# A planner's two cost constants: the price of an f32r product, and the rate of a load

## The chip, the cores and the metric

The kernel runs on one core of a Trainium2 chip. The core has five engines with queues of their own: PE multiplies matrices, DVE and ACT do vector work, POOL does a few small operations, and SP issues the transfers from memory. Each engine executes its queue strictly in the order in which it was written; semaphores hold an instruction back until its inputs are there and its output buffer is free. The metric is the device time of one execution in microseconds (us), the median of three.

## What is computed

Two layers of an encoder on 256 tokens of width 1024, all in float32. Layer 0 mixes with a Hyena convolution (long convolution by Fourier products) and cross attention, then a dense SwiGLU. Layer 1 mixes with dilated attention in three groups and cross attention, then a mixture of eight experts, of which each token takes two. That last part, in outline:

```
def moe_swiglu(h, router, wg, wu, wd):
    logits = jnp.dot(hf, router)
    top_v, top_i = lax.top_k(logits, TOP_K)          # TOP_K = 2 of 8 experts
    gates = jax.nn.softmax(top_v, axis=-1)
    ...
    for each expert e, on the tokens that chose it:
        y = (jax.nn.silu(x @ wg[e]) * (x @ wu[e])) @ wd[e]
    out[token] += gate * y
```

The widths are D = 1024 and DFF = 2816, so that an expert has 3 x 1024 x 2816 weights, 34.6 MB. The eight experts are 277 MB of the 373 MB that the kernel reads and writes.

## The kernel before

**Precision by three products.** A float32 product is made of three products of the faster type f32r: each operand is split into a high part (ACT casts it) and a low part (DVE subtracts the high part from the whole), and `mm3` multiplies high by high, high by low and low by high. So each weight passes through three engines before PE can use its low part: SP loads a *unit* (128 x 2048 floats, 1 MiB), ACT casts it in two halves of 128x1024, DVE makes the low half of each, and PE multiplies.

**An expert.** Its 33 units are used in blocks of six: four units of gate and up columns (48 products of 512 columns), then two units of the down matrix (24 products) for the block before. Between them lie `act`: SiLU on ACT, a product on DVE, four transposes of 128 columns on PE, and the split of their result by ACT and DVE (the cast to 128x512, called `aT` below). There are 8 x 33 = 264 such units, and they fill the second half of the run.

**The plan.** The kernel is not issued as it is written down. `Plan.add` records every operation with its duration by `Plan.cost`; `Plan.order` then plays the whole program forward with these durations, a list scheduler for five engines, a transfer queue, eight PSUM banks and 24 slots of 1 MiB in SBUF, and writes down in which order each engine starts its operations and which slot each buffer takes. `Plan.flush` emits the operations in that order. All of them are issued from one line (L299 of the profile), so the profile's groups are told apart by their tiles: `s` is a buffer in a slot, `b` a PSUM bank, `kt` holds the identity matrix for transposes (`b<-kt,s` is a transpose).

**What the durations decide.** At each moment of the played time an engine takes, of the operations that are ready and whose buffers fit, the one that is due first. A load is issued as soon as a slot can be spared (`fits`, the branch for kind "stream") and the played transfer queue holds less than BACKLOG = 6 us. A slot that is set free goes to the end of a list, and the next buffer takes the slot at its front. On the chip nothing of the played time is left except the orders and the slots: a load waits until the last user of its slot, as the plan has dealt it, is done. At most N_SPLIT = 4 slots hold split weights at a time.

The two prices that the change touches stand in `cost`: the load's bytes by 360e3 (bytes per us), and the f32r product's columns by 2.4 per ns and a fixed 2.5 ns.

Of the kernel before, what the change touches and what calls it, by code (L numbers as in the profile page):

```python
# [119 lines left out]
class _Eng:  # L120
# [3 lines left out]
    def __getattr__(self, fn):  # L124
# [3 lines left out]
LAT = {("tensor", "tensor"): 0.0, ("vector", "vector"): 0.07, ("scalar", "scalar"): 0.1, ("gpsimd", "gpsimd"): 0.1,  # L128
       ("scalar", "vector"): 0.13, ("vector", "scalar"): 0.17, ("scalar", "tensor"): 0.27, ("vector", "tensor"): 0.25}
FREE = 0.2  # L130
TABLES = {AF.Exp, AF.Silu, AF.Sin}
LOAD = 1.3
ISSUE, LAND = 1.2, 14.0
# [2 lines left out]
class Plan:  # L136
# [182 lines left out]
    def cost(self, eng, fn, a, kw, aps):  # L319

        n = max((self.width(x) for x in aps), default=1)
        if fn == "add_rows":
            return ISSUE
        if fn == "dma_start":
            ap = aps[0]
            return self.width(ap) * ap.ap[0][1] * 4 / 360e3
        if eng == "tensor":
            if fn == "transpose":
                return 0.109
            r = kw["rhs"]  # L330
            n = self.width(r.on(r.t.ref))
            if kw["rhs_dt"] == F32R:
                return max(0.107, 0.0025 + n * 0.4167e-3)
            return 4 * max(0.054, 0.0025 + n * 0.4167e-3)
        if eng == "scalar":
            ptr = isinstance(kw.get("scale"), View) + isinstance(kw.get("bias"), View)
            return 0.05 + 0.834e-3 * n + 0.2 * ("accum_out" in kw) + 0.09 * ptr
        if eng == "vector":
            return 0.07 + (6.4e-3 if fn == "reciprocal" else 1.04e-3) * n + 0.06 * (fn == "scalar_tensor_tensor")
        if kw.get("op") == OP.pow:  # L340
            return 0.35 + 0.16 * n
        return 0.05 + 2.3e-3 * n if fn == "tensor_tensor" else 0.05 + 3.5e-3 * n if fn == "tensor_copy" else 0.05
# [52 lines left out]
    def order(self):  # L395
# [35 lines left out]
        while done < len(ops):  # L431
# [23 lines left out]
            for e in engines:  # L455
# [36 lines left out]
                else:  # L492
# [3 lines left out]
                    f = op.args[2] if op.fn == "activation" else None  # L496
                    if f in TABLES and f != table:
                        table, end = f, end + LOAD
                        busy[e] = end
                heapq.heappush(events, busy[e])  # L500
                for m in op.mems:
                    m.left -= 1
                    m.end = max(m.end, end)
                    if not m.left and m.kind != "at" and not m.pinned:
                        heapq.heappush(frees, (m.end + FREE, len(out), len(frees), m))
                        heapq.heappush(events, m.end + FREE)
                        self.n_split -= m.split
# [1126 lines left out]
```

## Time and profile before

| | us |
|---|---|
| median of 3 runs | 1332.57 |
| lowest and highest | 1332.44, 1333.93 |
| the profiled execution | 1331.97 |
| its span in the trace | 1330.1 |

The span is cut in the trace at the first and the last instruction; 1.9 us of the execution lie around it. The rows quoted below are of this execution. The profile has a page (busy time of each engine, and the same in 40 slices of the span), a chain of waits (what the end waited for, followed back), lists of instructions by shape, lists of waits, windows (busy time and count of instructions in a stretch), and a timeline. A matmul's record in them lasts longer than the distance to the next one, since matmuls are pipelined: the pace of PE is read from counts over a stretch, not from the mean duration.

### The profile page before, as it was taken

The page shows a single profiled execution, that of the slowest core. Times are in us where ns is not written, and L with a number is a line of the kernel's source. Part 1 is how long each engine was busy: PE and PEld are TensorE (multiplying, and loading weights), DVE is VectorE, ACT ScalarE, POOL GpSimd, SP SyncE. Part 2 cuts the span into 40 slices and gives each one's busy share as a digit, 9 for nine tenths or more (in the row PEclk, how much of TensorE's full clock was granted, in tenths as well). Part 3 has the DMA queues.
Part 4 walks back from the last instruction along what each step waited for, and adds up shares of the span by engine and source line. Part 5 has one row for each costly group of instructions (what it writes and reads, how often), then busy time and mean ns, then how long its engine had stood idle before and what let it go on. Part 6 is the DMA issues. An engine that isn't in the chain of part 4 may idle for free.

```text
span 1330.1 us, 16843 instructions
## 1 busy us (share of the span) xinstructions
PE 1307.0 (98%) x6256; PEld 1073.6 (81%) x6256; DVE 1077.9 (81%) x1429; ACT 895.7 (67%) x1190; POOL 41.3 (3%) x38
## 2 busy tenths in 40 slices
PE   6999999999999999999999999999999999999997
PEld 4798888888878888888888888888888778777775
DVE  7989775554578777898999989999988888988886
ACT  7455754444566566687877777876876777777774
POOL 0100000000001000000000000000000000000000
PEclk9999999999999999999999999999999999999999
DMA  9548533357435456299999999999999999999992
GB/s 370 222 146 293 212 138 129 134 187 271 173 127 207 126 172 248 97 371 354 341 375 348 342 367 356 356 375 360 336 365 368 364 351 345 376 360 351 368 354 77
DMA packets 57437, 372.84 MB, mean 280 GB/s; under 512 B 6415, under 2 KB 10595, under 8 KB 13700
## 3 DMA queue, kind: packets, MB, share of 16 engines
q1 hardware_dynamic: 56196, 367.49, 73.8%
q0 software_dynamic: 1152, 4.19, 1.7%
q8 instruction: 51, 0.84, 0.2%
q14 instruction: 38, 0.31, 0.1%
HBM read 365.88 MB, written 5.79 MB: 279 GB/s over the span
## 4 chain that ended last, share of the span: by engine, by line
PE 88%; issue 7%; ACT 2%; DMA 1%; DVE 1%; SPq 0%; POOL 0%; POOLq 0%; ACTq 0%; DVEq 0%
PE b L299 88%; ACT s L299 2%; DVE s L299 1%; DMA out<-s,tiny 1%; DMA sm<-sm 0%; SPq L299 0%; POOL out L296 0%; POOLq L1375 0%; DVE tiny L299 0%; ACTq L299 0%; DVE cg L299 0%; POOLq L296 0%; DVEq L299 0%
## 5 line engine op out<-in xcount | busy, mean ns | idle before, releaser
L299 PE MATMUL b<-s,s 128*128 128x512 f32 (+1 forms) x5674 | 1279.0, 383 | 2.9 <-DVE s L299 0.9
L299 PEld LDWEIGHTS b<-s,s 128*128 128x128 f32 x5674 | 1003.9, 188 | 215.3 <-DVE s L299 15.0
L299 DVE TENSOR_TENSOR s<-s,s 128x1024 fp32r<-128x1024 f32 (+3 forms) x729 | 832.7, 1187 | 124.5 <-ACT s L299 123.6
L299 ACT CAST s<-s 128x1024 fp32r<-128x1024 f32 (+1 forms) x705 | 689.8, 1039 | 128.6 <-PE b L299 96.6
L299 DVE TENSOR_TENSOR s<-b,s 128x512 f32<-128x512 f32 (+5 forms) x206 | 123.0, 609 | 63.4 <-ACT s L299 58.9
L299 ACT CAST s<-b 128x512 fp32r<-128x512 f32 (+3 forms) x118 | 58.3, 504 | 130.5 <-PE b L299 127.4
L299 ACT ACTIVATE s<-b 128x512 f32<-128x512 f32 (+3 forms) x81 | 42.9, 539 | 68.7 <-PE b L299 68.6
L299 PE MATMUL b<-kt,s 128*128 128x128 f32 (+1 forms) x480 | 88.1, 273 | 1.2 <-DVE s L299 1.0
L299 PEld LDWEIGHTS b<-kt,s 128*128 128x128 f32 x480 | 65.1, 146 | 18.6 <-ACT s L299 2.2
L299 ACT ACTIVATE s<-b,tiny 128x512 f32<-128x512 f32 (+2 forms) x58 | 34.0, 611 | 28.0 <-PE b L299 20.7
L299 DVE SCALAR_TENSOR_TENSOR s<-b,sm,s 128x256 fp32r<-128x256 f32 (+1 forms) x88 | 38.0, 478 | 8.2 <-ACT s L299 6.6
L299 ACT ACTIVATE s<-b,sm 128x256 fp32r<-128x256 f32 (+1 forms) x84 | 35.2, 487 | 11.9 <-PE b L299 11.4
L296 POOL DMA_INDIRECT out<-s,tiny x8 | 14.4, 1794 | 761.3 <-ACT s L299 569.5
L299 POOL TENSOR_TENSOR tiny<-tiny,mhalf 128x1 f32<-128x1 f32 (+4 forms) x23 | 26.5, 1152 | 341.5 <-DVE tiny L299 327.1
L299 ACT ACTIVATE s<-x 128x512 f32<-128x512 f32 x16 | 10.1, 631 | 17.7 <-DVE x L299 13.5
L299 PE MATMUL b<-s 128*128 128x512 f32 (+4 forms) x40 | 11.9, 389 | 10.0 <-DMA s<-fw 5.9
L299 DVE TENSOR_TENSOR tiny<-tiny 128x1 f32<-128x1 f32 (+4 forms) x81 | 12.2, 156 | 10.2 <-ACT s L299 8.3
L299 DVE TENSOR_REDUCE tiny<-b 128x2 f32<-128x512 f32 (+3 forms) x25 | 12.3, 495 | 9.5 <-PE b L299 9.4
L299 DVE TENSOR_REDUCE tiny<-s 128x4 f32<-128x512 f32 (+3 forms) x26 | 13.9, 558 | 5.3 <-ACT s L299 5.3
L299 PEld LDWEIGHTS b<-s 128*128 128x128 f32 (+2 forms) x40 | 6.7, 195 | 11.6 <-DMA s<-fw 5.9
L299 DVE TENSOR_TENSOR x<-b,x 128x512 f32<-128x512 f32 x12 | 8.3, 691 | 9.1 <-PE b L299 9.0
L299 ACT COPY s<-b 128x512 f32<-128x512 f32 x11 | 6.3, 584 | 13.6 <-PE b L299 13.4
(65 smaller groups left out, 157.4 us busy)
## 6 DMA issues: line engine op xcount, KB each, us to landing
s<-w_moe SPq DMA_DIRECT2D x264, 1024.0 KB, 7.1
s<-w_ffn SPq DMA_DIRECT2D x33, 1024.0 KB, 4.9
s<-w_at SPq DMA_DIRECT2D x20, 1024.0 KB, 5.1
s<-w_kv SPq DMA_DIRECT2D x8, 1024.0 KB, 7.9
s<-w_hy SPq DMA_DIRECT2D x8, 1024.0 KB, 16.3
s<-w_out SPq DMA_DIRECT2D x8, 1024.0 KB, 4.9
s<-mem SPq DMA_DIRECT2D x4, 512.0 KB
out<-x SPq DMA_DIRECT2D x3, 512.0 KB
```

What stands on the lines that cost most here:

```text
L296: self.nc.gpsimd.indirect_dma_start(out=out, out_offset=bass.IndirectOffsetOnAxis(ap=index, axis=0), in_=rows, in_offset=None, compute_op= ...
L299: getattr(getattr(self.nc, op.eng), op.fn)(*args, **kw)
```

## The change

Three lines. The fixed part of an f32r product goes from 2.5 to 13.7 ns, and its floor from 107 to 110 ns: 512 columns cost 227.05 ns in place of 215.85, 256 columns 120.4 in place of 109.2. A load costs its bytes by 390e3 in place of 360e3 per us: a unit of 1,048,576 bytes 2.689 us in place of 2.913. No operation is added, removed or changed; the orders and the slots are what the plan makes of these numbers.

```
+RATE = 390e3
...
         if fn == "dma_start":
             ap = aps[0]
-            return self.width(ap) * ap.ap[0][1] * 4 / 360e3
+            return self.width(ap) * ap.ap[0][1] * 4 / RATE
...
             if kw["rhs_dt"] == F32R:
-                return max(0.107, 0.0025 + n * 0.4167e-3)
+                return max(0.11, 0.0137 + n * 0.4167e-3)
             return 4 * max(0.054, 0.0025 + n * 0.4167e-3)
```

Every engine's order differs nearly everywhere. Two places of the last expert show it; the lines count from L299 before and L300 after, since one line was added. Behind a buffer's slot number stands a running number that is given out as the instructions are written.

The first place is ACT, around the cast of a block's transposes (128x512, from a bank). The casts to 128x1024 are of weights: on the right of the arrow stands the unit that was loaded. Before:

```order
L299 CAST s2_10348<-s20_10274 128x1024
L299 CAST s11_10354<-s20_10274 128x1024
L299 CAST s15_10365<-b7_74 128x512
L299 CAST s18_10370<-s6_10296 128x1024
L299 CAST s0_10377<-s6_10296 128x1024
L299 CAST s4_10389<-s8_10316 128x1024
```

After:

```order
L300 CAST s16_10375<-s2_10118 128x1024
L300 CAST s9_10385<-s2_10118 128x1024
L300 CAST s1_10393<-s14_10147 128x1024
L300 CAST s10_10402<-s14_10147 128x1024
L300 CAST s7_10414<-b1_68 128x512
L300 CAST s15_10418<-s21_10165 128x1024
L300 CAST s11_10426<-s21_10165 128x1024
```

Two things have moved. The unit behind the 128x512 cast was loaded 74 running numbers ahead of its cast before (10296 to 10370) and 253 ahead after (10165 to 10418); a unit takes some 20 of them, so that is 3 to 4 units ahead before and about 13 after. And the casts that stand in front of the 128x512 cast are further ahead of PE, which the second place shows.

The second place is PE, from the last transpose of the same block (`b<-kt`) to the first product with the weights that are cast next behind the 128x512 cast (s18_10370 before, s15_10418 after). Before:

```order
L299 MATMUL b7_74<-kt_77,s1_10277 128x128
L299 MATMUL b6_73<-s2_10348,s14_8883 128x512
L299 MATMUL b6_73<-s2_10348,s22_8916 128x512
L299 MATMUL b6_73<-s2_10348,s14_8883 128x512 x2
L299 MATMUL b6_73<-s2_10348,s22_8916 128x512
L299 MATMUL b6_73<-s11_10354,s14_8883 128x512 x2
L299 MATMUL b6_73<-s11_10354,s22_8916 128x512
L299 MATMUL b6_73<-s11_10354,s14_8883 128x512 x2
L299 MATMUL b6_73<-s11_10354,s22_8916 128x512
L299 MATMUL b6_73<-s18_10370,s14_8883 128x512 x2
```

After:

```order
L300 MATMUL b1_68<-kt_77,s13_10333 128x128
L300 MATMUL b3_70<-s16_10375,s4_9029 128x512
L300 MATMUL b3_70<-s16_10375,s20_9044 128x512
L300 MATMUL b3_70<-s9_10385,s4_9029 128x512 x2
L300 MATMUL b3_70<-s9_10385,s20_9044 128x512
L300 MATMUL b3_70<-s9_10385,s4_9029 128x512 x2
L300 MATMUL b3_70<-s9_10385,s20_9044 128x512
L300 MATMUL b0_67<-s1_10393,s7_10414 128x512 x3
L300 MATMUL b4_71<-s1_10393,s7_10414 128x512 x3
L300 MATMUL b0_67<-s10_10402,s7_10414 128x512 x3
L300 MATMUL b4_71<-s10_10402,s7_10414 128x512 x3
L300 MATMUL b0_67<-s15_10418,s7_10414 128x512 x3
```

Before, 11 products lie between the last transpose and the first product that needs weights cast behind it; after, 20.

## Rows read from the trace of the kernel before

**Rows 1.** The page: busy time, share and instructions of PE; its granted clock in slices.

```profile
PE 1307.0 (98%) x6256; PEld 1073.6 (81%) x6256; DVE 1077.9 (81%) x1429; ACT 895.7 (67%) x1190; POOL 41.3 (3%) x38
...
PEclk9999999999999999999999999999999999999999
```

**Rows 2.** The chain of waits in order of time: start us, us, what.

```profile
57.77 1.03 ACT s L299 x2
58.82 1.27 DVE s L299 x3
...
102.30 1.05 ACT s L299
...
103.40 928.16 PE b L299 x4457
...
1061.08 14.64 PE b L299 x64
...
1076.23 1.06 ACT s L299
1077.31 1.24 DVE s L299
1078.59 14.68 PE b L299 x64
```

**Rows 3.** Windows: length, busy us (count) by engine, PEclk, DMA share, GB/s.

```profile
575.00:1000.00 425.00, 425.00 (x1956) 352.48 (x1955) 386.05 (x394) 329.64 (x378) 8.18 (x4) 1.00 0.95 358
1000.00:1300.00 300.00, 298.05 (x1331) 237.79 (x1330) 259.79 (x264) 217.86 (x253) 4.63 (x3) 1.00 0.96 360
...
10.00:40.00 30.00, 28.70 (x112) 18.97 (x113) 28.60 (x71) 25.25 (x48) 2.27 (x4) 1.00 1.02 417
1040.00:1050.00 10.00, 9.73 (x45) 7.68 (x44) 8.50 (x9) 6.69 (x9) 0.00 (x0) 1.00 1.01 428
```

**Rows 4.** PE by shape, 318 to 358 us: xcount, busy us, mean ns, idle us.

```profile
L299 PE MATMUL b<-s,s 128*128 128x512 f32 x178 | 40.5, 389 | 0.0
```

**Rows 5.** The same, 575 to 1000 us.

```profile
L299 PE MATMUL b<-s,s 128*128 128x512 f32 x1784 | 417.1, 392 | 0.0
```

**Rows 6.** The same, 1000 to 1300 us.

```profile
L299 PE MATMUL b<-s,s 128*128 128x512 f32 x1223 | 294.7, 396 | 2.0 <-DVE s L299 0.7
```

**Rows 7.** Waits, 1000 to 1300 us: who <- whom, us, times, longest.

```profile
ACT s L299 <- PE b L299: 83.1, 37, 4.5
...
PEld b L299 <- DVE s L299: 12.4, 28, 0.7
```

**Rows 8.** Timeline of one block: start us, us, engine, operation, count, [idle before <-releaser].

```profile
1288.89 0.27 PE L299 MATMUL b<-kt,s 128*128 128x128 f32 x1
...
1289.20 0.59 ACT L299 CAST s<-b 128x512 fp32r<-128x512 f32 x1 [3.66 <-PE b L299]
1289.68 3.89 ACT L299 CAST s<-s 128x1024 fp32r<-128x1024 f32 x4
...
1292.04 5.31 PEld L299 LDWEIGHTS b<-s,s 128*128 128x128 f32 x24 [0.54 <-DVE s L299]
...
1297.72 0.30 PEld L299 LDWEIGHTS b<-s,s 128*128 128x128 f32 x2 [0.36 <-DVE s L299]
```

**Rows 9.** DMA issues, 575 to 1000 us: xcount, KB each, us to landing.

```profile
s<-w_moe SPq DMA_DIRECT2D x143, 1024.0 KB, 7.3
```

**Rows 10.** ACT by shape, 575 to 1000 us: the casts of weights.

```profile
L299 ACT CAST s<-s 128x1024 fp32r<-128x1024 f32 x300 | 295.1, 1050 | 23.9 <-PE b L299 17.7 <-DVE s L299 5.7
```

**Rows 11.** Waits of SP's queue, 575 to 1000 us.

```profile
SPq L299 <- PE b L299: 230.5, 96, 5.2
SPq L299 <- DVE s L299: 136.4, 75, 4.3
```

**Rows 12.** Waits of SP's queue, 1000 to 1300 us.

```profile
SPq L299 <- DVE s L299: 158.9, 74, 4.0
SPq L299 <- PE b L299: 97.0, 40, 5.2
```

More of the change, by code (lines that the diff above doesn't have):

```diff
@@ L130 @@
 FREE = 0.2
+RATE = 390e3
 TABLES = {AF.Exp, AF.Silu, AF.Sin}
@@ L325, in cost @@
             ap = aps[0]
-            return self.width(ap) * ap.ap[0][1] * 4 / 360e3
+            return self.width(ap) * ap.ap[0][1] * 4 / RATE
         if eng == "tensor":
@@ L332, in cost @@
             if kw["rhs_dt"] == F32R:
-                return max(0.107, 0.0025 + n * 0.4167e-3)
+                return max(0.11, 0.0137 + n * 0.4167e-3)
             return 4 * max(0.054, 0.0025 + n * 0.4167e-3)
```

## The prediction

> **What bounds the kernel now.** The page comes first: PE is busy for 98% of the span, at the higher of its two clocks, 2.4 GHz, in every slice [rows 1] (1.00 in the windows [rows 3]). So PE is the bound, and only its gaps and its pace can be won or lost. The chain of waits says where gaps are: after some waits in the first 103 us it is PE without a break from 103.40 to 1031.56 us (4457 products), and from there it breaks about once in 15 us, each time with an ACT and a DVE instruction of weight-split length in the break (1076.23, 1077.31), before PE goes on for 64 products [rows 2].
>
> Since a busy PE is not yet PE at its pace, I count products. The stretch from 318 to 358 us holds nothing but 512-column products: 178 in 40.5 us, 227.5 ns each [rows 4]. That is the new constant (227.05), not the old one (215.85). From 575 to 1000 us there are 1956 PE instructions in 425 us, 1784 of them of 512 columns [rows 3, 5]: 1784 x 227.5 ns = 405.9 us, which leaves 19.1 us for the 172 small ones, 111 ns each. From 1000 to 1300 us there are 1331 in 300 us, 1223 of 512 columns [rows 3, 6]: 278.3 us, and 108 small ones at 111 ns make 12.0, together 290.3. **9.7 us of these 300 are lost**, on the measure of the stretch before, and both stretches are the same work, experts.
>
> Why there? In the second stretch PE's weight loads wait 28 times for DVE, 12.4 us in all [rows 7], a wait that the first stretch doesn't list at all. One block shows the ring: the last transpose starts at 1288.89; ACT has idled 3.66 us for it and casts it at 1289.20, and only behind it, at 1289.68, come the casts of the next weights; PE gets the low half at 1292.04, after 0.54 us of waiting, and waits again for 0.36 at 1297.72 [rows 8]. From the transpose to 1292.04 are 3.15 us, and PE has 11 products to fill them, 2.5 us. ACT could have cast those weights earlier, had the order let it.
>
> **What the change does, part by part.** Nothing is computed otherwise; the plan's view of the experts turns over. A block of six units is 72 products and four transposes. By the old prices PE needs 72 x 0.2158 + 4 x 0.109 = 16.0 us for it, and the loads 6 x 2.913 = 17.5: the plan thinks that loads bound, runs its stock of loaded units down, and casts each just before its use. By the new prices PE needs 72 x 0.2271 + 4 x 0.11 = 16.8 us and the loads 6 x 2.689 = 16.1: PE bounds, the slots stay full, casts run ahead. The order bears this out at the end of the program: the unit behind the transposes' cast is loaded 3 to 4 units ahead before, about 13 ahead after, and PE has 20 products to cover that cast where it had 11.
>
> *The pace of loads.* The trace shows the old plan's draining on the chip: from 575 to 1000 us 143 units are loaded [rows 9] and 150 are cast (300 halves) [rows 10], so the stock falls by 7. It falls because of the slots that the plan has dealt, not because transfers are slow: SP's queue waits 230.5 + 136.4 of the 425 us for PE and DVE, that is for slots [rows 11], and 158.9 + 97.0 of 300 afterwards [rows 12]. To feed PE without a gap, 6 units in 16.8 us, takes 374 GB/s. The long stretches show 358 and 360, but the stretch from 10 to 40 us shows 417 and that from 1040 to 1050, in the midst of the experts, 428 [rows 3]. So 374 can be had when loads are issued earlier, and the 13 units of stock would cover a shortfall: at 360 GB/s a block's loads take 17.5 us, 0.7 more than PE, so that the stock loses a unit in four blocks and 13 units last 52 blocks, while all experts together have 264/6 = 44. Cost of the loads' part: nothing, hidden by that stock.
>
> The Trainium skill (DMA: Bandwidth & Descriptors, section Bandwidth, Where 436 GB/s comes from) says that for transfers from HBM the limit of some 358 GB/s per core binds. By that rule the two long stretches were at the limit and the change could not speed the experts up at all; this is the second rival below, which stands on rows 3 alone. The same skill (HBM Reference, Specifications (TRN2)) says that a core that streams alone reaches about 425, and this kernel runs alone; the 417 and 428 of the trace agree.
>
> *PE's and ACT's orders in the experts.* 20 products are 4.5 us against the 3.15 us of the ring, so the gap closes. What remains is what the first stretch shows, where the old plan still had its stock: the 111 ns for small instructions contain it. So the stretch from 1000 to 1300 us gets 9.7 us shorter. The bounds are +0 (the stalls stay) and about 12.4 (the whole wait for DVE [rows 7]); I take 9.7 because it is counted against the same work with a stock of loaded units. The rest of the experts after 1300 us goes on in the same way and I leave it out.
>
> *Everything before 575 us.* The price of PE moves every order there too. From 103 us on the chain is PE alone [rows 2], so there is next to nothing to win. In the first 103 us three breaks are in the chain, 1.03 + 1.27 and 1.05 us [rows 2], 3.3 in all: these can go, or as many of the same size can arise. I take 0, with 3 us to either side.
>
> *Pace.* The product's price in the plan doesn't change its time: 227.5 ns before and after. The skill (TensorE: Matmul & The Clock Gate, Back-to-back issue gap) gives N/2.4 + 2.5 ns for a warm, isolated product, 216 for 512 columns, the old constant. By that the new plan would be the one that misjudges PE; rows 4 decide for 227.5.
>
> **The sum.** The profiled execution took 1331.97 us; less 9.7 is 1322.3. The median of the runs lies 0.6 above the profiled one, so 1322.9, with 3 us either way: 1319.5 to 1326.
>
> **Rivals.**
>
> 1. *The stalls go only in part.* The ring from a transpose through ACT and DVE is in the new order too, and not every block has 20 products in it; where it has 11 to 14, PE can wait as it does now. For it: the orders are made by a scheduler that knows no fixed distance. Against: the old order has distances as short (9 products at the least) between 575 and 1000 us too, where the stock is larger, and the rows show no wait from them. If half of the 9.7 us stays: 1327.7.
>
> 2. *The transfers are the bound.* If 358 to 360 GB/s are all that a long stretch yields, the units come no sooner than now, the stock only shifts the gaps to the end, and PE waits for loads instead of DVE. For it: 358 and 360 over 425 and 300 us, at a DMA share of 0.95 and 0.96 [rows 3]. Against: the waits of SP's queue for slots [rows 11, 12], and 417 and 428 in the shorter stretches [rows 3]. It gives 1332, no change.
>
> 3. *The slots become the bound (slower).* With 13 to 14 loaded units in 24 slots, and 4 with split weights, few are left for an expert's activations. Then a cast or a SiLU on ACT waits for its slot, that is for a DVE or PE instruction that is late by plan, and all casts of weights queue behind it on ACT; PE waits in every block from the first expert on, not only from 1000 us. Price: the 9.7 us now lost are in 1223/72 = 17 blocks, 0.57 us each; if all 44 blocks lose that, 25.1 us take the place of 9.7, +15.4, 1348. It decides against the change from the point at which more than 17 of the 44 blocks wait as long as now. Against: in the old plan the stock is as large shortly after 575 us (it falls by 7 units until 1000 us [rows 9, 10], to 3 or 4), and PE has no break there [rows 2].
>
> That the change does nothing is ruled out by the orders.
>
> **How the numbers follow.** What a measurement of this kernel can tell from no change is 0.2%, 2.7 us: faster means under 1329.9. My forecast, 1319.5 to 1326: 0.71. Rival 1, 1326 to 1329.5: 0.13. Rival 2, 1330 to 1334: 0.09. Rival 3, above 1335: 0.07. Faster is the forecast and rival 1, 0.84; no change is rival 2, 0.09; slower is rival 3, 0.07. The range for 8 in 10 takes in the forecast and most of rival 1: 1318.5 to 1329.5.
>
> **What would show it.** Right: the chain is PE without a break from some 100 us to the end of the experts; from 1000 to 1300 us PE executes about 1375 instructions (1331 x 300/290.3) where it executed 1331; weight loads no longer wait for DVE there; the loads run at 370 to 375 GB/s in long stretches, and loaded units and cast units keep step. Rival 1: the wait for DVE is still listed, at some 6 us. Rival 2: the loads stay at 360 GB/s, and ACT or PE waits for transfers near the end. Rival 3: ACT waits for PE or DVE in every block from 575 us on. Wrong in a way that I have not priced: the breaks of the first 103 us grow by more than 3 us.

## The result, and the profile after

The changed kernel takes 1325.87 us (median of 4 runs, 1325.09 to 1326.87), beside 1333.05 us for the kernel before: a ratio of 0.9946, 95% interval 0.9929 to 0.9963. That is 7.2 us less; 9.7 were forecast. Run again later, it took 1325.09 beside 1333.24 (0.9941, 0.9928 to 0.9955). The profiled execution took 1326.87 us with a span of 1325.0, so the two profiles lie only 5.1 us apart.

The page after, PE's busy time and its granted clock in slices, beside [rows 1]:

```profile
PE 1304.2 (98%) x6256; PEld 1076.4 (81%) x6256; DVE 1083.5 (82%) x1429; ACT 907.6 (68%) x1190; POOL 43.1 (3%) x38
...
PEclk9999999999999999999999999999999999999999
```

The chain of waits after (start us, us, what), beside [rows 2]:

```profile
12.86 49.40 PE b L300 x252
62.34 292.57 PE b L300 x1473
...
357.66 1.47 POOL tiny L300
...
378.51 2.71 POOL tiny L300
...
383.95 190.56 PE b L300 x1009
574.51 613.43 PE b L300 x2812
```

Two things are to be seen. The breaks from 1031 us on are gone: PE runs from 574.51 to 1187.94 without one, and where the chain goes over to other engines behind that, PE stays busy all the same (300.00 of the 300 us up to 1300, below). The breaks of the first 103 us are gone too; the prediction counted three, but its rows are three instructions in two breaks. But there are two that the kernel before does not have, around 357 and 380 us, and in both a POOL instruction is the longest piece. PE itself idles for less than the chain is away from it: 0.39 us in the first, 0.88 and 0.19 us in the second.

The windows of the experts after (length, busy us and count of PE, PEld, DVE, ACT, POOL, then PEclk, DMA share, GB/s), beside [rows 3]:

```profile
575.00:1000.00 425.00, 425.00 (x1950) 350.41 (x1949) 387.15 (x396) 332.03 (x375) 6.48 (x4) 1.00 0.96 370
1000.00:1300.00 300.00, 300.00 (x1370) 246.64 (x1368) 271.43 (x273) 236.04 (x265) 4.76 (x3) 1.00 0.89 347
```

PE's 512-column products after, from 318 to 358, 575 to 1000 and 1000 to 1300 us (count, busy us, mean ns, idle us), beside [rows 4 to 6]:

```profile
L300 PE MATMUL b<-s,s 128*128 128x512 f32 x178 | 40.5, 389 | 0.0
...
L300 PE MATMUL b<-s,s 128*128 128x512 f32 x1775 | 416.9, 392 | 0.0
...
L300 PE MATMUL b<-s,s 128*128 128x512 f32 x1262 | 295.5, 392 | 0.0
```

The pace is what it was: 178 in 40.5 us. From 1000 to 1300 us PE now executes 1370 instructions where it executed 1331. By the prediction's measure (227.5 ns each for 1262, 111 ns for the other 108) that is 299.1 us of work in 300, so 0.9 are lost where 9.7 were.

The waits from 1000 to 1300 us after (who <- whom, us, times, longest), beside [rows 7]:

```profile
ACT s L300 <- PE b L300: 30.4, 45, 3.1
...
PEld b L300 <- DVE s L300: 0.8, 5, 0.2
```

The weight loads waited 12.4 us for DVE there before, and 0.8 now. A block late in the program (start us, us, engine, operation, count), beside [rows 8]:

```profile
1269.83 0.38 PE L300 MATMUL b<-kt,s 128*128 128x128 f32 x2
1270.08 11.93 PEld L300 LDWEIGHTS b<-s,s 128*128 128x128 f32 x53
1270.08 12.12 PE L300 MATMUL b<-s,s 128*128 128x512 f32 x52
1272.48 0.57 ACT L300 CAST s<-b 128x512 fp32r<-128x512 f32 x1
1272.95 1.05 ACT L300 CAST s<-s 128x1024 fp32r<-128x1024 f32 x1
```

The cast behind the transposes starts 2.7 us after they did and the weight cast behind that one at 1272.95; PE goes through 52 products without noticing either.

Loads and weight casts from 575 to 1000 us after, beside [rows 9, 10]:

```profile
s<-w_moe SPq DMA_DIRECT2D x148, 1024.0 KB, 7.6
...
L300 ACT CAST s<-s 128x1024 fp32r<-128x1024 f32 x296 | 297.8, 1051 | 78.6 <-DVE s L300 43.8 <-PE b L300 34.1
```

148 units are loaded and 296 halves, that is 148 units, are cast: the stock no longer falls. SP's queue still waits for slots (251.6 us for PE and 109.1 for DVE, beside [rows 11]), and the transfers give 370 GB/s where they gave 358.

To cut each trace in two I use one mark that all kernels have, four small products of the router (16x8 in the list), which stand close to the start of the experts. Before and after (start us, us, engine, operation, count):

```profile
548.69 0.61 PE L299 MATMUL b<-kt,s 16*128 16x8 f32 x4
```

```profile
551.16 0.61 PE L300 MATMUL b<-kt,s 16*128 16x8 f32 x4
```

Up to the mark the changed kernel is 2.5 us **later** (551.16 - 548.69). Behind it the span has 773.8 us left where it had 781.4 (1325.0 - 551.16 and 1330.1 - 548.69): 7.6 us shorter. The two make up the 5.1 us between the profiles.

### The profile page after: what moved, and what is told of

Its sections match the earlier page's. It is cut to its first block, busy times and chain, and to the rows that moved or that the text cites. A ratio compares the mean times of both kernels' runs of the same rounds, so it can differ in the third digit from the quotient of the medians.

```text
span 1325.0 us, 16885 instructions
## 1 busy us (share of the span) xinstructions
PE 1304.2 (98%) x6256; PEld 1076.4 (81%) x6256; DVE 1083.5 (82%) x1429; ACT 907.6 (68%) x1190; POOL 43.1 (3%) x38
## 4 chain that ended last, share of the span: by engine, by line
PE 88%; issue 7%; DVE 2%; DMA 2%; ACT 1%; POOL 0%; SPq 0%; POOLq 0%; DVEq 0%; ACTq 0%
PE b L300 88%; DVE s L300 2%; ACT s L300 1%; DMA out<-s,tiny 1%; DMA kt<-consts 1%; POOL tiny L300 0%; DVE tiny L300 0%; SPq L300 0%; POOL out L297 0%; DVE x L300 0%; POOLq L1376 0%; POOLq L297 0%; DVEq L300 0%; ACTq L300 0%
## 5 line engine op out<-in xcount | busy, mean ns | idle before, releaser
L300 PE MATMUL b<-s,s 128*128 128x512 f32 (+3 forms) x5676 | 1275.5, 382 | 5.1 <-ACT s L300 4.1
L300 PEld LDWEIGHTS b<-s,s 128*128 128x128 f32 (+1 forms) x5676 | 1007.0, 188 | 211.2 <-issue 6.7
L300 DVE TENSOR_TENSOR s<-s,s 128x1024 fp32r<-128x1024 f32 (+2 forms) x732 | 840.0, 1185 | 137.1 <-ACT s L300 133.7
L300 ACT CAST s<-s 128x1024 fp32r<-128x1024 f32 (+2 forms) x705 | 704.3, 1038 | 250.0 <-PE b L300 145.6
L300 DVE TENSOR_TENSOR s<-b,s 128x512 f32<-128x512 f32 (+5 forms) x206 | 123.1, 607 | 31.9 <-ACT s L300 27.7
L300 ACT CAST s<-b 128x512 fp32r<-128x512 f32 (+3 forms) x118 | 58.6, 504 | 55.1 <-PE b L300 53.1
L300 PE MATMUL b<-kt,s 128*128 128x128 f32 (+1 forms) x480 | 86.2, 277 | 1.2 <-DMA kt<-consts 0.6
L300 PEld LDWEIGHTS b<-kt,s 128*128 128x128 f32 x480 | 65.1, 148 | 19.9 <-issue 2.4
L300 ACT ACTIVATE s<-b 128x512 f32<-128x512 f32 (+3 forms) x81 | 43.3, 538 | 15.2 <-PE b L300 10.2
L300 ACT ACTIVATE s<-b,tiny 128x512 f32<-128x512 f32 (+2 forms) x58 | 33.7, 609 | 27.3 <-DVE tiny L300 16.3
L300 ACT ACTIVATE s<-b,sm 128x256 fp32r<-128x256 f32 (+1 forms) x84 | 34.6, 481 | 17.6 <-PE b L300 17.0
L300 DVE SCALAR_TENSOR_TENSOR s<-b,sm,s 128x256 fp32r<-128x256 f32 (+1 forms) x88 | 38.0, 477 | 10.6 <-ACT s L300 10.5
L300 POOL TENSOR_TENSOR tiny<-tiny,mhalf 128x1 f32<-128x1 f32 (+4 forms) x23 | 29.8, 1295 | 341.2 <-DVE tiny L300 341.2
L300 ACT ACTIVATE s<-x 128x512 f32<-128x512 f32 x16 | 10.1, 631 | 19.5 <-DVE x L300 13.7
L300 DVE TENSOR_REDUCE tiny<-b 128x2 f32<-128x512 f32 (+3 forms) x25 | 12.4, 495 | 11.8 <-PE b L300 11.7
L300 DVE TENSOR_TENSOR tiny<-tiny 128x1 f32<-128x1 f32 (+4 forms) x81 | 12.7, 158 | 9.6 <-POOL tiny L300 5.4
L300 DVE TENSOR_REDUCE tiny<-s 128x4 f32<-128x512 f32 (+3 forms) x26 | 14.2, 557 | 3.3 <-ACT s L300 3.3
L300 PE MATMUL b<-s 128*128 128x512 f32 (+3 forms) x38 | 11.0, 367 | 5.9 <-DMA s<-fw 5.9
L300 DVE TENSOR_TENSOR x<-b,x 128x512 f32<-128x512 f32 x12 | 8.2, 690 | 9.0 <-PE b L300 8.9
L300 DVE TENSOR_TENSOR s<-b,tiny 128x512 f32<-128x512 f32 (+3 forms) x26 | 13.9, 560 | 0.3
L300 ACT ACTIVATE s<-s,tiny 128x256 f32<-128x256 f32 (+1 forms) x24 | 13.0, 583 | 1.3 <-DVE tiny L300 1.3
```

The costliest lines, as they stand in the source:

```text
L300: getattr(getattr(self.nc, op.eng), op.fn)(*args, **kw)
```

## The experiments

The theory has two parts. (a) The late gain comes from the plan no longer letting the stock of loaded units run out; whichever price eases the balance of a block will do. (b) The front lost time by its new order, with POOL's powers in the two new breaks. All kernels at a glance; the ratio is to the kernel before, run in the same job (a job is a set of kernels run together), and the last two columns are the mark in the profiled execution and the rest of its span.

| kernel | median us | ratio | interval | to the mark | rest |
|---|---|---|---|---|---|
| before | 1333.05 | 1 | | 548.7 | 781.4 |
| after | 1325.87 | 0.9946 | 0.9929 to 0.9963 | 551.2 | 773.8 |
| new_late | 1323.92 | 0.9936 | 0.9920 to 0.9953 | 549.6 | 772.6 |
| new_early | 1334.91 | 1.0013 | 1.0004 to 1.0023 | 550.1 | 783.4 |
| rate_only | 1322.62 | 0.9928 | 0.9911 to 0.9944 | 549.5 | 771.5 |
| price_only | 1325.07 | 0.9952 | 0.9935 to 0.9968 | 549.4 | 773.2 |
| rate330 | 1343.99 | 1.0078 | 1.0061 to 1.0095 | 552.4 | 791.1 |
| after_gap | 1326.69 | 0.9944 | 0.9927 to 0.9960 | 552.0 | 773.8 |
| before_gap | 1334.17 | 1.0004 | 0.9994 to 1.0014 | 549.7 | 782.1 |
| rate_only_gap | 1322.94 | 0.9920 | 0.9903 to 0.9936 | 549.3 | 771.7 |
| after_gap320 | 1324.62 | 0.9935 | 0.9918 to 0.9952 | 548.4 | 773.6 |
| after_again | 1325.09 | 0.9941 | 0.9928 to 0.9955 | 550.5 | 773.9 |
| gap320_again | 1323.99 | 0.9933 | 0.9920 to 0.9947 | 549.2 | 773.7 |
| rate_again | 1322.59 | 0.9925 | 0.9912 to 0.9939 | 549.1 | 771.7 |

### The change in two halves

The new prices for the experts alone, and, as the mirror image, for everything ahead of them alone (new_early has the two pairs of numbers exchanged). The edit of new_late against the kernel before, without the two lines of `cost` that read these numbers:

```diff
+RATE, FIXED = 360e3, 0.0025
...
+        plan.rate, plan.fix0 = 390e3, 0.0137
         self.moe_layer()
```

> The new rate and product price for the experts' operations alone (those recorded from the expert layer on); everything recorded ahead of it keeps the old ones, and the first 2660 of 6216 PE operations stand exactly as in the kernel before. Theory (late gain and front loss are separate, and the late gain is the stock of raw units): from 1000 us on PE loses 2 to 3 us as in the changed kernel where the kernel before loses 12, and the front costs what it costs before: 1333.0 - 9.5 + 1 = 1324.5, 1323 to 1325.5, at or under the changed kernel's 1325.9. Rival (the late gain needs the front's new order, or the transfers bind): 1330 or more.

> The mirror image: the new rate and price ahead of the experts, the old ones for the experts' operations; the first 2486 PE operations stand exactly as in the changed kernel. Theory: the stock of raw units drains as in the kernel before, PE waits for DVE from some 1000 us on (12 us there), and the front is the changed kernel's, whose loss at 376 to 388 us is 3.7 us when the long power on POOL falls there: 1333 + 0 to 3 = 1333 to 1336. Rival (the front's order carries part of the gain of 7.2 us): under 1331. If the long power is an accident of one execution, its profile shows no break at 381 us and the time stays near 1333.

Measured: 1323.92 and 1334.91 us. The windows from 1000 to 1300 us, of new_late and then of new_early (columns as above):

```profile
1000.00:1300.00 300.00, 300.00 (x1372) 247.85 (x1371) 273.21 (x275) 238.14 (x266) 4.76 (x3) 1.00 0.89 344
```

```profile
1000.00:1300.00 300.00, 297.96 (x1332) 237.88 (x1331) 259.65 (x263) 216.51 (x252) 4.63 (x3) 1.00 0.95 360
```

The whole gain sits in the experts' prices, and comes without a single PE operation of the first 2660 moved: 1372 instructions, rest 772.6. The front's new order by itself loses a little: new_early is slower than before by 0.04 to 0.23%. In their profiles the mark comes at 548.7 to 549.7 us with the front of before (before, new_late, before_gap) and at 550.1 to 551.2 with the changed one (new_early, after, after_again). Both parts of the theory held; by these numbers the half of the change that lies ahead of the experts costs 1 to 2 us. They do not all say so: price_only, whose front is nearly that of the changed kernel, reaches the mark at 549.4 us. The section on the powers shows what it is spared.

### One price at a time

rate_only and then price_only, each as an edit of the changed kernel that takes the other price back:

```diff
-                return max(0.11, 0.0137 + n * 0.4167e-3)
+                return max(0.107, 0.0025 + n * 0.4167e-3)
```

```diff
-RATE = 390e3
+RATE = 360e3
```

> The kernel before with 390 instead of 360 bytes per ns and the old product price. A block of six units is then 16.0 us of PE against 16.1 us of loads in the plan. Theory (what counts is that the plan does not let the stock drain, whichever price does it): its plan keeps 13 to 14 raw units to the end, late stalls gone: 1323 to 1327. Rival (the product price is what matters, since it is PE that was modelled too fast): about 1333, the same as before.

> The kernel before with the new product price and the old 360 bytes per ns: 16.8 us of PE against 17.5 us of loads a block. Theory: the plan's stock falls only to 9 to 13 units by the end of its 44 blocks, so the late stalls are gone here too: 1323 to 1328. Rival (only the rate counts, since it is the loads that the plan thought late): 1331 to 1334.

Measured: 1322.62 and 1325.07 us, both as the stock theory has it. The windows from 1000 to 1300 us of rate_only and of price_only:

```profile
1000.00:1300.00 300.00, 300.00 (x1372) 248.35 (x1371) 276.33 (x276) 238.42 (x265) 5.22 (x3) 1.00 0.89 345
```

```profile
1000.00:1300.00 300.00, 300.00 (x1373) 247.97 (x1372) 271.67 (x275) 233.22 (x266) 5.06 (x3) 1.00 0.93 356
```

Either price alone is enough. rate_only keeps a product price that the trace shows to be 12 ns too low (215.85 against 227.5), and no kernel here is faster. So the prices need not be right. Nor need PE become the bound in the plan: by the sums in the two expectations a block's loads still take longer than its products, by 0.1 us in rate_only and by 0.7 in price_only, where they take 1.5 longer in the kernel before. What matters is whether the plan's stock lasts. Over 44 blocks 0.7 us make 31 us, less than the 41 us of PE work that the next expectation gives to the stock of 14 units; 1.5 us make 66 and use it up. (These are estimates from the plan's prices.)

### The dose

```diff
-RATE = 390e3
+RATE = 330e3
```

> The changed kernel with a rate of 330 bytes per ns in place of 390. A block is then 16.8 us of PE against 19.1 us of loads in the plan, 2.3 us short, so the plan's 14 units (41 us of PE work) are gone after 18 blocks, at some 880 us, earlier than the 1000 us of the kernel before (1.5 us short a block). Theory (stock): PE loses from there what the kernel before loses from 1000 us, 9.5 us in 300, so 13 us in 420, with the weight loads waiting for DVE and ACT for PE: 1333 + 4 + 0 to 3 for the front = 1337 to 1340. Rival (the stock does not matter, a calibrated product price is enough): 1326.

Measured: 1343.99 us, 4 us above the upper end of the stock theory, and 18 above the rival. Windows of rate330 (columns as far as PE: length, PE busy and count, PEclk, DMA share, GB/s):

```profile
700.00:800.00 100.00, 100.00 (x469) 1.00 0.94 347
800.00:900.00 100.00, 99.66 (x450) 1.00 0.96 357
900.00:1000.00 100.00, 98.73 (x453) 1.00 0.94 350
```

and its waits from 1000 to 1300 us:

```profile
ACT s L300 <- PE b L300: 79.4, 37, 3.2
...
PEld b L300 <- DVE s L300: 14.9, 29, 0.8
```

PE begins to idle between 800 and 900 us, as the count of the stock had it (880), and the same waits as in [rows 7] are back, 14.9 us of the weight loads where before had 12.4. The rest of the span is 9.7 us longer than before's, where I had 4. I had let each block lose as much as in the kernel before, and only more blocks lose; but from 1000 to 1300 us, with 1320 instructions, 1212 of them of 512 columns, 12.3 us are lost by the prediction's measure where before lost 9.7. The front is a changed one again, with the mark at 552.4 us. The transfers run at 347 to 357 GB/s in this kernel and at 370 in the changed one. So the pace of the transfers is set by when the plan issues them; 358 was no limit.

### POOL's powers in the front

What ends the new breaks? DVE and POOL around 378 us, before and then after (start us, us, engine, operation, count, idle before and its releaser):

```profile
377.41 1.22 DVE L299 TENSOR_TENSOR s<-s,s 128x1024 fp32r<-128x1024 f32 x1
378.55 0.17 DVE L299 TENSOR_SCALAR tiny<-tiny 128x8 f32<-128x8 f32 x1
378.79 1.65 POOL L299 TENSOR_TENSOR tiny<-tiny,mhalf 128x8 f32<-128x8 f32 x1 [18.01 <-DVE tiny L299]
```

```profile
378.26 0.17 DVE L300 TENSOR_SCALAR tiny<-tiny 128x8 f32<-128x8 f32 x1
378.48 1.23 DVE L300 TENSOR_TENSOR s<-s,s 128x1024 fp32r<-128x1024 f32 x1
378.51 2.69 POOL L300 TENSOR_TENSOR tiny<-tiny,mhalf 128x8 f32<-128x8 f32 x1 [18.45 <-DVE tiny L300]
```

The three instructions are the same, but the subtraction (two operands in SBUF, 1.23 us) has changed places with the short instruction that feeds the power. It starts 0.03 us ahead of the power, and the power takes 1.04 us longer. This holds without exception in the fourteen traces: in 56 cases the 128x1024 subtraction began between 232 ns ahead of a power and 31 ns behind it, and each of these powers took 854 to 1106 ns more than its short time; in 140 cases it began 92 ns or more behind it, while it ran, and the power took its short time, to within 60 ns. The Trainium skill (SBUF — State Buffer, section Who interferes with whom) has the rule: a DVE instruction with two SBUF inputs contends with a GpSimd instruction that reads SBUF, and the one that comes later is blocked. The trace agrees for POOL as the later one. It does not for DVE as the later one: that subtraction takes its 1.2 us all the same (378.48 in the third trace below).

The test puts one more DVE instruction between the two, with no other order moved; it sums a constant into a tile of its own, which nothing reads:

```diff
                 self.emit(op, ...)
+                if op.kind == "gap":
+                    self.nc.vector.tensor_reduce(self.gap[:, 4:5], self.gap[:, :1].to_broadcast([128, 128]), axis=AX.X, op=OP.add)
```

> The changed kernel with the same order on every engine, but for one more instruction on DVE behind each of the 23 tensor_scalar that make the power's input: a sum of 128 columns, some 0.2 us. It lets the power on POOL start ahead of the 128x1024 subtraction that now starts 0.04 us ahead of it at 378.5 us. Theory (a power that starts while DVE subtracts from SBUF two operands waits for it to end; that makes the break at 381 us, the break at 360 us and the lower clock behind it): the powers at 357.7 and 378.5 us take 0.55 and 1.65 us in place of 1.46 and 2.69, both breaks and the fall of the clock are gone: 1325.9 - 3.7 = 1322, 1321.5 to 1323.5. Rival (the long power has another cause, or the break comes from the plan's order whatever POOL does): 1326, or more for the 23 instructions (at most 4.6 us of DVE).

> The same 23 sums in the kernel before, as a control. There the power at 378.8 us starts ahead of any such subtraction and takes 1.65 us already, and the longest power, 2.7 us at 46.1 us, is followed by work that PE has. Theory: no break of PE ends on POOL, so nothing is to be had and DVE has room: 1333, within 1.5 us. Rival (the extra instruction helps or hurts by itself): it moves by the same 3 to 4 us as in the changed kernel, or up by some.

> The kernel before with the rate of 390 alone (1322.6) and the 23 sums. Its powers at 357 and 379 us are short already. Theory: 1322.6, within 1 us, about as fast as the changed kernel with the sums; what is left is the start and the switches, which neither touches. Rival (the powers at 47 and 160 us cost too): 1321 or less.

Measured: 1326.69, 1334.17 and 1322.94 us. The controls stay where they were, so the sums cost nothing that can be measured. after_gap missed its own aim: the subtraction began 0.02 us behind the power (379.45 and 379.43 us), the power took 2.75 us, and the break stayed. It separates nothing; a longer sum does:

```diff
-                    self.nc.vector.tensor_reduce(self.gap[:, 4:5], self.gap[:, :1].to_broadcast([128, 128]), axis=AX.X, op=OP.add)
+                    self.nc.vector.tensor_reduce(self.gap[:, 4:5], self.gap[:, :1].to_broadcast([128, 320]), axis=AX.X, op=OP.add)
```

> The changed kernel with the 23 sums made over 320 columns in place of 128: with 128 the subtraction behind the sum began 0.02 us after the power at 379.4 us and the power still took 2.75 us, and so did the one at 358.2 us (1.65). With 320 it begins about 0.2 us after it; in all traces so far a power that began 0.135 us or more ahead of a subtraction took its short time. Theory (a power waits for a subtraction from two SBUF operands that began before it or just with it; the break of PE at 381 us, that at 360 us and the lower clock hang on it): 0.55 and 1.65 us, no break, no fall of the clock: 1325.9 - 3.7 = 1322, 1321 to 1323.5. Rival (the break belongs to the order and stays when POOL is quick): 1326 or more. DVE gives at most 23 x 0.4 = 9 us, which the control of 128 columns in the kernel before showed to cost nothing.

DVE and POOL of after_gap320 at the same place:

```profile
378.08 0.48 DVE L598 TENSOR_REDUCE gap<-gap 128x1 f32<-128x320 f32 x1
378.25 1.65 POOL L300 TENSOR_TENSOR tiny<-tiny,mhalf 128x8 f32<-128x8 f32 x1 [18.78 <-DVE tiny L300]
378.48 1.22 DVE L300 TENSOR_TENSOR s<-s,s 128x1024 fp32r<-128x1024 f32 x1
```

The power is back at 1.65 us, the one at 357 us at 0.55, and the mark comes at 548.4 us in place of 551.2. Of PE's idle 0.88 and 0.19 us around 382 us the 0.88 are gone. The break at 360 us did not go, against the expectation; PE's first products behind it in after and in after_gap320, with the idle time ahead of them:

```profile
361.18 0.44 PE L300 MATMUL b<-kt,s 128*128 128x128 f32 x2 [0.39 <-ACT s L300]
```

```profile
360.92 0.44 PE L300 MATMUL b<-kt,s 128*128 128x128 f32 x2 [0.70 <-ACT s L300]
```

With the power short, the chain there leads over two of the sums (0.39 us each) and a subtraction (1.13 us). The median is 1324.62, less of a gain than the 1322 expected. So the pair was run once more, with rate_only beside it:

> The changed kernel as it is, beside the next two on one chip, since they differ from it by 0.1 to 0.3%. 1325.1 to 1326.9 as in its first four executions, with the power at 378.5 us at 2.69 us and the clock down behind the break.

> The changed kernel with the 23 sums of 320 columns. Theory (the long power is worth the break and part of the clock): 1 to 3 us under after_again, 1323 to 1325, with the power at 1.65 us and a break of some 0.3 us at 382 us. Rival (the order alone makes the loss, or the sums eat the gain): within 0.5 us of after_again.

> The kernel before with the rate of 390 alone. Theory (late stage as in the changed kernel, front as in the kernel before, where the power at 379 us starts ahead of the subtraction): 1322.4 to 1323.0, 2.5 to 4 us under after_again. Rival (the difference between the two was one of chips): within 1 us of after_again.

Measured: 1325.09, 1323.99 and 1322.59 us. The sums save 1.1 us here, at the lower end of what the theory allowed, and the intervals of the two ratios overlap. The changed kernel was not in the job before; its two medians, 1325.87 and 1325.09, lie 1.2 and 0.5 us above the 1324.62 of after_gap320. That the powers cost something is shown by the traces; in the medians it is known to about a microsecond. rate_only is 2.5 us below the changed kernel on the same chip, and all its five times (1322.16 to 1323.68) lie under all five of the changed kernel (1324.48 to 1326.17). But the theory for it, a late stage as in the changed kernel, did not hold: in the profiles 1.4 us of the lead lie ahead of the mark (549.1 and 550.5) and 2.2 behind it (771.7 and 773.9).

What the sums do not cure is the clock. Windows from 381 to 385 us of after_again, gap320_again, rate_again (the first alone) and price_only (columns as in the first windows):

```profile
381.00:383.00 2.00, 1.00 (x3) 0.27 (x3) 2.00 (x5) 1.10 (x2) 0.00 (x0) 1.00 0.00 0
383.00:385.00 2.00, 1.80 (x8) 1.38 (x8) 2.00 (x4) 0.00 (x0) 0.00 (x0) 0.60 0.00 0
```

```profile
381.00:383.00 2.00, 1.84 (x6) 0.81 (x5) 2.00 (x4) 1.11 (x2) 0.00 (x0) 0.68 0.00 0
383.00:385.00 2.00, 2.00 (x8) 1.62 (x7) 1.21 (x3) 0.69 (x1) 0.00 (x0) 0.50 0.00 1
```

```profile
381.00:383.00 2.00, 2.00 (x10) 0.80 (x8) 1.87 (x6) 2.00 (x3) 0.00 (x0) 1.00 0.01 2
```

```profile
381.00:383.00 2.00, 1.00 (x4) 0.09 (x2) 1.92 (x7) 1.54 (x2) 0.00 (x0) 1.00 0.02 8
383.00:385.00 2.00, 1.78 (x9) 1.32 (x10) 2.00 (x3) 0.15 (x1) 0.00 (x0) 1.00 0.00 0
```

In the changed kernel PE idles for half of the first window, and the granted clock falls to 0.60 in the second. In gap320_again that break is gone (1.84 of 2 us busy), and the clock still falls, to 0.50 of full speed, that is 1.2 GHz. In the execution of after_gap320 that was profiled it stayed at 1.00 there. And price_only has the same break (1.00 of 2 us busy) and keeps its clock at 1.00. So the break neither makes the fall by itself nor is needed for it. The fall is in six of the eight traces with the changed front or nearly that front, and in none of the six with the front of before or nearly that. What brings it on is open.

What each of the two costs can be read from the eight traces, since from PE's first instruction behind the break at 360 us to the mark it executes the same 986 instructions (985 in the trace of new_early) in nearly the same order. They take 189.4 to 190.0 us in the five traces with the break at 381 us and the fall, 188.7 in gap320_again (fall alone), 188.4 in price_only (break alone) and 187.4 in after_gap320 (neither). So the break that the long power makes costs about 1 us and the fall of the clock 1.0 to 1.6, together at most 2.6, where the expectations reckoned with 3.7.

The times agree. Where executions of one kernel differ in their mean clock, the one at 0.998 is the faster: 1324.24 us in after_gap, beside 1326.54 to 1327.51 at 0.996 and 0.997, and 1332.44 in new_early, beside 1334.13 to 1336.14 at 0.995 to 0.997. That one time of new_early is no longer than those of the kernel before. The mean also takes in the end of the run, where the clock falls in every trace, so 0.997 alone tells little; it is 0.996 or 0.997 in all nine executions of the changed kernel, 0.998 in five of nine with the long sums, and 0.998 or 0.999 in all nine of rate_only.

## Why the prediction was right, and where it was not

**The late breaks** were the main term, and its mechanism held: stock drained by the plan, casts just in time, weight loads waiting for DVE. The mechanism's marks came as listed: 1370 instructions from 1000 to 1300 us (about 1375 forecast), 0.8 us of weight loads waiting for DVE, 370 GB/s (370 to 375), loads and casts in step. One sign did not come: the chain is not PE alone from some 100 us on, because of the two new breaks at 357 and 380 us. new_late, rate_only, price_only and rate330 move the late breaks on and off by the plan's balance alone. That PE bounds in the plan, as the prediction has it, is more than is needed; a stock that lasts will do. The term's size was 9.7 us, by the stretch from 1000 to 1300 us; there it came to 8.8 (9.7 less the 0.9 that remain). Over all that follows the mark it is 7.6: from 575 to 1000 us PE executes 1950 instructions, 1775 of them of 512 columns, 423.2 us by the same measure, so that 1.8 are lost in a stretch that I had taken as the one without loss. With the fronts and prices of new_late and rate_only the rest is 1.2 and 2.3 us shorter still; which detail of the experts' order makes these two was not tried.

**Everything before 575 us** is the step whose mechanism failed: "there is next to nothing to win", so 0, with 3 us either way for the first 103 us. The breaks there did go, but I never asked what an order could lose where PE had no break yet. It cost a break of about 1 us behind the long power at 378.5 us, and, in both profiles of the changed kernel, had a fall of the clock that costs 1.0 to 1.6. The rows for the power were in the trace of before. Its POOL powers of 128x8 take 1.65 us at 378.8 us, but 2.67 at 46.1, while the plan counts 0.35 + 0.16 x 8 = 1.63; that is a price which depends on the neighbour on another engine, and every new order deals it anew. Nothing in the trace of before announced the fall.

**How the sum came out.** The mark came 2.5 us later in the first pair of profiles and 1.8 in the second. Some 0.9 of that is the start of the one profile of before: new_late and before_gap have the same front and reach the mark at 549.6 and 549.7 us, though from the end of their last early break (103.40 us in before, 104.53 and 104.35 in these) to the mark all three take 445.1 to 445.3 us. So 7.6 less 2.5, the 5.1 us between the two profiles, makes the front look too bad: these two executions lie 1.1 us below and 1.0 above the medians of their kernels. With the medians' 7.2 us, 7.6 for the late breaks leave 0.4 for the front. Of the 2.5 us that are missing from the 9.7, 2.1 then belong to the late term, which was too large (7.6 by the profiles), and 0.4 to the front; how much the front lost is known to no better than 0.4 to 2.5 us. The centre of the forecast, 1322.9, was 3 us too low, and 1325.87 lies 0.1 us inside the upper end of the range, so that the range held is in part luck.

**Pace**: 178 products in 40.5 us before and after, as said.

**Rival 1**, stalls that go only in part, would have left some 6 us of weight loads waiting for DVE; 0.8 are left. Its number, 1327.7, lies nearer to the result than the forecast's 1322.9, by chance: what it says would stay has gone. **Rival 2**, the transfers as the bound, falls by 370 GB/s over 425 us, and by rate330, in which the plan issues the same transfers later and they run at 347 to 357 GB/s. **Rival 3**, slots, falls too: PE idles nowhere from 575 to 1000 us, although ACT now waits longer ahead of the weight casts (78.6 us in place of the 23.9 of [rows 10]); that is time in which it is ahead.

**The fastest kernel** of the study is also the smallest edit, the rate alone: 1322.59 us, 0.9925 (0.9912 to 0.9939); with the sums added it measures the same.

## What to carry to other kernels

In a planner that orders both loads and compute, sum its own prices over one block of the steady stage, and ask how far it believes the loads to fall short and how many blocks its stock will bear that. Here 1.5 us a block drained a stock of 14 units and cost 8 us long after; 0.7 us a block cost nothing. Price a change of a global constant stage by stage, and apply it to the stage that needs it; an order that already runs without a break has little to win by being dealt again, and can lose. And where the same instruction has two durations in a trace, find out what it meets in the slow cases, before a new order moves it there.

## What the runs showed of the hardware

A power on POOL of 128 x 1 to 8 elements takes 0.55 to 1.65 us, and 0.85 to 1.11 us more if a 128x1024 DVE subtraction with both operands in SBUF began up to 232 ns before it or up to 31 ns behind it; begun 92 ns or more behind it, the subtraction disturbs it no more, and is not delayed itself. The loads of one core, alone on the chip, ran at 370 GB/s over 425 us, where the kernel before got 358. TensorE's granted clock went to 1.2 GHz for some 3 us around 384 us behind a break of about 1 us in five traces, and in one without such a break; in price_only it stayed at 2.4 GHz behind the same break. The fall cost 1.0 to 1.6 us.
